# Scores of two heads in one step, with the low-part query products on the two row halves of the array

## The chip, the cores and the metric

The kernel runs on one core of a Trainium2 chip. The metric is device time in microseconds (us) from the start to the end of one execution. Where a trace is quoted, it comes from one profiled execution of the program.

## The reference

One layer of a hybrid encoder, for 1024 prompt frames and 64 frames that continue a stream with 512 cached frames. Every frame is normalised and projected to two attention branches and gates. Each branch has 8 heads of 64 channels. What the change touches are the scores, query times key over the 64 channels of a head, in both branches. Everything is float32.

```python
# stick-breaking branch ("sb")
z = jnp.einsum("bqhd,bkhd->bhqk", q, k).astype(jnp.float32) * ATTN_SCALE
causal = k_pos[None, :] < q_pos[:, None]
log_beta = jax.nn.log_sigmoid(z)
log_keep = jnp.where(causal, jax.nn.log_sigmoid(-z), 0.0)
suffix = lax.cumsum(log_keep, axis=3, reverse=True) - log_keep
w = jnp.where(causal, jnp.exp(log_beta + suffix), 0.0)
return jnp.einsum("bhqk,bkhd->bqhd", w.astype(v.dtype), v)
# band branch ("cb"): keys of the last 8 chunks of 64, softmax with a bias by distance
s = jnp.einsum("...qhd,...khd->...hqk", q, k).astype(jnp.float32) * ATTN_SCALE
```

Then both branch outputs are gated, projected, merged, projected again and added to the input.

## The kernel before, in words

**Split numbers.** A fast float32 product (the type `float32r`) keeps only part of the digits. So weights, activations, queries and keys are split into a high part and a low part, and a product is a sum of partial products. For the scores of one head the keys stand with the 64 rows of their high part and the 64 rows of their low part on the 128 rows of the array (tile `ks`, or `kss` for the 64 sample frames). The queries' high part stands twice, on both row halves, and so does their low part (tile `sq`, four planes: high and low of head 0, high and low of head 1). One matmul of 128 rows with the high part (line 725) gives high times high plus high times low; a second one with the low part (line 726) adds low times high plus low times low. Both go to the same PSUM tile `z` of one bank. `ks` and `sq` are filled by DMAs that `place_k` and `place_q` issue on SP's queue, `place_q` with four per tile.

**Phases.** Phase 1 (up to about 267 us of the trace) makes the normalised input and the natural-layout groups (line 357). Phases 2 and 3 (about 267 to 866 us) are one pipeline over all attention units, in which the matmuls of the remaining projections stand as fillers: `run_fill` and then `proj_units` give one filler matmul at a time (lines 563 and 661, up to 384 columns each). Phases 4 and 5 (to the end) are the rest of the projections and the output.

**Order of the attention pipeline.** The order on each engine is the order in which the program is written (`manual_schedule`). `seq` lists branch, pair of heads, query tile and head; query tile 8 is the 64 sample frames, tiles 0 to 7 have 128 prompt frames. A step is one query tile of one head. In step i, `qk(i)` computes the scores. Their width is 128 keys per query tile so far in the first branch (128 to 1024), 128 to 640 in the band branch, 576 for the sample frames. Widths over 512 are computed in two halves, in turn, with a `z` tile each; there are three `z` tiles. In the first branch ScalarE makes two sigmoids of each `z` (lines 728 and 729, tiles `kp` and `be`); in the band branch VectorE adds the bias and finds the extreme (line 731) and ScalarE takes the exponential (line 735). Then come half of the step's fillers, a pending `av` (values times weights, line 817, whose two heads stand on the two column halves of the array), `tr(i - 2)` (transposes of the weights, line 777, two PSUM tiles `pt`), `mid(i)` (first branch: the scan and a multiplication on VectorE, lines 745 and 746; band branch: the division, line 749), and the other half of the fillers. The number of fillers of a step follows the width of its scores.

**Buffers around it.** `be` has 3 buffers, `kp` 2, the band branch's small tile `sm` 4, `z` 3, `pt` 2. At the start of `qk` GpSimd writes one column of `kp` (line 716), which must wait until the buffer's former user is done. On GpSimd's queue the low parts of the filler weights (line 98) stand behind that.

Of the kernel before, what the change touches and what calls it, by code (L numbers as in the profile page):

```python
# [18 lines left out]
NP = 1024  # L19
# [11 lines left out]
def hybrid_step_kernel(ctx: ExitStack, tc: tile.TileContext, x_prompt, x_sample, c_sbk, c_sbv, c_cbk, c_cbv,  # L31
# [420 lines left out]
    def alloc_q(key, ci):  # L452
        if ci == 3:
            SQ[key, 3] = am.tile([128, 4, 64], F32R, name="sqs", bufs=1)
        else:
            n = min(CH[ci][1], NP) - CH[ci][0]
            SQ[key, ci] = am.tile([128, 4, n], F32R, name=f"sq{ci}", bufs=2 if ci == 2 else 1)
        return SQ[key, ci]
# [228 lines left out]
    def until(j):  # L687
        while prog[0] < j:
            next(gen)

# [1 line left out]
    seq = [(b, p, t, hd) for b in ("sb", "cb") for p in range(NPAIR) for t in [8] + list(range(8))  # L692
           for hd in range(2)]
# [9 lines left out]
    def qk(i):  # L703
        b, p, t, hd = seq[i]
# [4 lines left out]
        be = am.tile([128, NP], F32, name="be", bufs=3)  # L709
# [4 lines left out]
        if b == "sb":  # L714
            kp = ax.tile([128, NP + 2], F32, name="kp", bufs=2)
            G.memset(kp[:r, n:n + 1], 0.0)
        else:
            kp = am.tile([128, 4], F32, name="sm", bufs=4)
            bt = BI[2 * p + hd]
            off = 0 if t == 8 else 640 - n  # L720
        for j, (x, y) in enumerate(hs):
            z = psZ.tile([128, 512], F32, name="z")
            o = k0 * 128
            m = y - x
            TE.matmul(z[:r, :m], s[:, 2 * hd, q0:q0 + r], ks[:, hd, o + x:o + y], start=True, stop=False)  # L725
            TE.matmul(z[:r, :m], s[:, 2 * hd + 1, q0:q0 + r], ks[:, hd, o + x:o + y], start=False, stop=True)  # L726
            if b == "sb":
                A.activation(kp[:r, x:y], z[:r, :m], AF.Sigmoid, scale=-0.125)  # L728
                A.activation(be[:r, x:y], z[:r, :m], AF.Sigmoid, scale=0.125)
            else:  # L730
                V.tensor_tensor_reduce(be[:r, x:y], z[:r, :m], bt[:r, off + x:off + y], 1.0,  # L731
                                       BIG if j == 0 else kp[:r, j - 1:j], OP.add, OP.min, kp[:r, j:j + 1])
        if b == "cb":
            j = len(hs) - 1
            A.activation(be[:r, :n], be[:r, :n], AF.Exp, bias=kp[:r, j:j + 1], scale=-1.0, accum_out=kp[:r, 2:3])  # L735
        st[i] = (be, kp)

    def mid(i):
        b, p, t, hd = seq[i]
        r = rows(t)  # L740
        k0, n = band(b, t)
        be, kp = st[i]
        if b == "sb":
            im = imp[0:64, 960 - n:960] if t == 8 else imp[:, NP - n:NP]
            V.tensor_tensor_scan(kp[:r, n - 1::-1], kp[:r, n - 1::-1], im[:, ::-1], 0.0, op0=OP.mult, op1=OP.add)  # L745
            V.tensor_tensor(out=be[:r, :n], in0=be[:r, :n], in1=kp[:r, 1:n + 1], op=OP.mult)  # L746
# [9 lines left out]
    def tr(i):  # L756
        b, p, t, hd = seq[i]
        r = rows(t)
        k0, n = band(b, t)
        be, _ = st.pop(i)  # L760
# [64 lines left out]
    def prefetch(b, p, t):  # L825
        """Loads for the pair after (b, p), spread over its query tiles."""
# [38 lines left out]
    tot = {b: sum(wt[b](band(b, t)[1]) for bb, p, t, hd in seq if bb == b) for b in ("sb", "cb")}  # L865
    amount = {"sb": n_sb, "cb": n_cb}
    acc, emitted = 0.0, 0
    LAG = 2
    avq = []
    for i in range(len(seq) + LAG + 1):  # L870
        m = 0
        if i < len(seq):
            b, p, t, hd = seq[i]
            if b == "sb" and t == 8 and hd == 0:
                until(UK[p])
            if b == "cb" and p == 0 and t == 8 and hd == 0:
# [5 lines left out]
            qk(i)  # L882
            if hd == 0:
                prefetch(b, p, t)
            acc += amount[b] * wt[b](band(b, t)[1]) / tot[b]
            if (b, p, t) == ("cb", 0, 8):
                acc += 12
# [3 lines left out]
        fill(m // 2)  # L891
        while avq:
            av(*avq.pop(0))
        if 0 <= i - LAG < len(seq):
            tr(i - LAG)
            b, p, t, hd = seq[i - LAG]
            if hd == 1 and (t % 2 == 1 or t == 8):
# [129 lines left out]
```

## Time and profile before

| | |
|---|---|
| time, 3 runs | 1035.23, 1035.96 (median), 1036.86 us |
| span of the profiled execution | 1034.6 us |
| TensorE busy | 1014.8 us, 98% |
| weight loads busy (PEld) | 968.4 us, 94% |
| VectorE / ScalarE / GpSimd busy | 53% / 40% / 25% |
| granted TensorE clock | 0.999 |

The times lie some 1.4 us above the span, which runs from the first to the last instruction. Matmul durations in the profile are modelled from issue to the end of the drain, so consecutive ones overlap; how long a matmul holds the array is read from the distance between two starts. PE is TensorE's matmul, PEld its weight load, DVE is VectorE, ACT is ScalarE, POOL is GpSimd. Shapes such as `128*128 128x384` are weight rows times weight columns, and then the output.

### The profile page before, as it was taken

How to read it: one execution, taken by the hardware profiler on the slowest of the kernel's cores; microseconds unless marked ns; L12 is line 12 of the kernel's file. 1: busy time of each engine (PE TensorE's matmuls, PEld its weight loads, DVE VectorE, ACT ScalarE, POOL GpSimd, SP SyncE). 2: the span in 40 equal slices, each digit the busy share in tenths (PEclk: the TensorE clock that was granted, in tenths of full speed). 3: DMA queues.
4: the chain of work that ended last, by engine and by line, in shares of the span. 5: the costliest groups of instructions: out<-in, count | busy, mean ns of one | idle time of the engine just before them, and what ended most of it. 6: DMA issues, size and time to landing. Idle time of an engine off the chain costs nothing.

```text
span 1034.6 us, 19354 instructions
## 1 busy us (share of the span) xinstructions
PE 1014.8 (98%) x7412; PEld 968.4 (94%) x7412; DVE 543.9 (53%) x1069; ACT 418.7 (40%) x942; POOL 255.2 (25%) x277
## 2 busy tenths in 40 slices
PE   6999999999999999999999999999999999999998
PEld 5999999999999989999999999998988898999998
DVE  5416656402476556657655645565557685674111
ACT  5534443212454435444444454444445433552000
POOL 3227666202221111212121111101103211453110
PEclk9999999999999999999999999999999999999999
DMA  7654453745547323723384354665576834554322
GB/s 237 213 187 151 163 191 128 267 136 165 160 112 192 96 69 102 206 60 95 92 211 122 107 144 131 165 169 161 162 204 185 224 92 139 187 163 149 101 93 71
DMA packets 159660, 155.23 MB, mean 150 GB/s; under 512 B 23184, under 2 KB 144912, under 8 KB 159440
## 3 DMA queue, kind: packets, MB, share of 16 engines
q1 hardware_dynamic: 142800, 136.17, 44.2%
q10 hardware_dynamic: 16768, 17.83, 5.7%
q8 instruction: 58, 0.95, 0.4%
q14 instruction: 34, 0.28, 0.1%
HBM read 90.77 MB, written 49.81 MB: 136 GB/s over the span
## 4 chain that ended last, share of the span: by engine, by line
PE 91%; SPq 3%; DMA 2%; DVE 1%; ACT 1%; issue 1%; POOL 0%; ACTq 0%; DVEq 0%
PE acc L563 33%; PE acc L357 18%; PE acc L661 9%; PE o L817 7%; PE pt L777 6%; PE z L726 3%; PE z L725 3%; PE acc L992 3%; PE acc L991 3%; PE acc L990 3%; SPq L49 2%; DMA wrawx<-in_w_in_dram 1%; PE pk L301 1%; PE pt L229 1%; DMA d_ccbT<-hc 1%
## 5 line engine op out<-in xcount | busy, mean ns | idle before, releaser
L563 PE MATMUL acc<-xh,whi 128*128 128x384 f32 (+1 forms) x768 | 255.5, 333 | 0.1
L563 PE MATMUL acc<-xh,wlo 128*128 128x384 f32 (+1 forms) x768 | 255.3, 332 | 0.0
L563 PE MATMUL acc<-xl,whi 128*128 128x384 f32 (+1 forms) x768 | 254.8, 332 | 0.0
L98 POOL TENSOR_TENSOR wlo<-wraw,whi 128x1024 fp32r<-128x1024 f32 x51 | 127.6, 2501 | 440.2 <-ACT whi L91 386.1
L563 PEld LDWEIGHTS acc<-xh,wlo 128*128 128x128 f32 x768 | 144.8, 189 | 1.3
L563 PEld LDWEIGHTS acc<-xl,whi 128*128 128x128 f32 x768 | 144.5, 188 | 1.3
L563 PEld LDWEIGHTS acc<-xh,whi 128*128 128x128 f32 x768 | 144.5, 188 | 1.2 <-ACT sg L550 0.3
L745 DVE TENSOR_TENSOR_SCAN kp<-kp,imp 64x576 f32<-64x576 f32 (+8 forms) x72 | 110.6, 1536 | 5.1 <-ACT kp L728 5.1
L735 ACT ACTIVATE be<-be,sm 128x640 f32<-128x640 f32 (+5 forms) x72 | 50.8, 706 | 106.6 <-DVE sm L731 106.4
L728 ACT ACTIVATE kp<-z 128x384 f32<-128x384 f32 (+6 forms) x112 | 53.8, 480 | 97.3 <-PE z L726 87.6
L777 PE MATMUL pt<-ident,be 128*128 128x128 f32 (+2 forms) x608 | 88.8, 270 | 0.9 <-DVE wT L788 0.6
L786 ACT ACTIVATE wT<-pt 128x512 f32<-128x512 f32 (+3 forms) x104 | 52.9, 509 | 82.5 <-PE pt L777 81.6
L788 DVE COPY wT<-pt 128x256 f32<-128x256 f32 (+3 forms) x104 | 46.0, 442 | 70.3 <-PE pt L777 69.9
L777 PEld LDWEIGHTS pt<-ident,be 128*128 128x128 f32 (+2 forms) x608 | 68.7, 139 | 11.6 <-issue 7.1
L357 PE MATMUL acc<-whi,xh 128*128 128x256 f32 x256 | 75.2, 296 | 0.0
L357 PE MATMUL acc<-wlo,xh 128*128 128x256 f32 x256 | 71.7, 282 | 0.0
L357 PE MATMUL acc<-whi,xl 128*128 128x256 f32 x256 | 71.5, 281 | 0.0
L357 PE MATMUL acc<-whix,xh 128*128 128x256 f32 x256 | 70.9, 279 | 0.0
L357 PE MATMUL acc<-whix,xl 128*128 128x256 f32 x256 | 70.6, 278 | 0.0
L91 ACT ACTIVATE whi<-wraw 128x1024 fp32r<-128x1024 f32 x52 | 55.0, 1059 | 38.4 <-DVE y L996 35.8
L357 PE MATMUL acc<-wlox,xh 128*128 128x256 f32 x256 | 70.5, 277 | 0.0
L746 DVE TENSOR_TENSOR be<-be,kp 64x576 f32<-64x576 f32 (+8 forms) x72 | 62.3, 865 | 8.8
(157 smaller groups left out, 2168.7 us busy)
## 6 DMA issues: line engine op xcount, KB each, us to landing
wraw<-in_w_in_dram SPq DMA_DIRECT2D x40, 512.0 KB, 4.9
sq<-hl SPq DMA_DIRECT2D x32, 192.0 KB, 4.5
sq<-d_qT SPq DMA_DIRECT2D x32, 192.0 KB, 3.6
xt<-in_x_prompt_dram SPq DMA_DIRECT2D x8, 512.0 KB, 5.6
wrawx<-in_w_in_dram SPq DMA_DIRECT2D x8, 512.0 KB, 4.3
d_kT<-hl SPq DMA_DIRECT2D x8, 512.0 KB, 4.7
d_qT<-hl SPq DMA_DIRECT2D x8, 512.0 KB, 4.8
ks<-d_kT SPq DMA_DIRECT2D x16, 256.0 KB, 4.6
```

Source lines behind the costliest of these rows:

```text
L91: A.activation(h, raw, AF.Copy)
L98: (eng or G).tensor_tensor(out=l, in0=raw, in1=h[:].bitcast(F32), op=OP.subtract)
L357: TE.matmul(ps, x, w, start=m == 0, stop=m == len(steps) - 1)
L563: TE.matmul(ps[:, :b - a], w[:, k], xk(x, k)[:, a:b], start=k == 0 and n == 0, stop=k == KT - 1 and n == 2)
L661: TE.matmul(ps[:, :n], w[:, p, cw], g[:, a:e], start=p == 0 and m == 0, stop=p == NPAIR - 1 and m == 2)
L728: A.activation(kp[:r, x:y], z[:r, :m], AF.Sigmoid, scale=-0.125)
L735: A.activation(be[:r, :n], be[:r, :n], AF.Exp, bias=kp[:r, j:j + 1], scale=-1.0, accum_out=kp[:r, 2:3])
L745: V.tensor_tensor_scan(kp[:r, n - 1::-1], kp[:r, n - 1::-1], im[:, ::-1], 0.0, op0=OP.mult, op1=OP.add)
L746: V.tensor_tensor(out=be[:r, :n], in0=be[:r, :n], in1=kp[:r, 1:n + 1], op=OP.mult)
L777: TE.transpose(pt[:kr, x, :r], be[:r, kb * 128:kb * 128 + kr], ident[:r, :r])
L786: A.activation(w[:, sl:sl + m, q0:q0 + r], pt[:, :m, :r], AF.Copy)
L817: TE.matmul(o[hd * 64:hd * 64 + 64, c0:c1], vv[:kr, kb, hd * 64:hd * 64 + 64], wT[b, p, j, hd, s // 4][:kr, s % 4, c0:c1], start=si == 0, ...
```

## The change

A step now takes one query tile of both heads of a pair, so `seq` has 72 steps instead of 144. Of each part of the scores, first both heads' high-part products are issued, each on all 128 rows into a `z` tile of its own. Then come both low-part products, each on 64 rows only: low queries times the high part of the keys. Head 0 takes rows 0 to 63 of the array, head 1 rows 64 to 127. The product low times low is no longer computed. For this, `place_k` puts the high keys of head 1 on the lower row half, and `sq` has three planes, of which the third holds the low parts of both heads, one on each row half; `place_q` issues five DMAs instead of four, with three quarters of the bytes.

`qk` is a generator. Its first part runs at the start of a step, its second part (the second half of a wide tile, and the exponentials of the band branch) in the middle. A step's fillers stand in four groups, with `av`, the transposes of head 0 of the step before, the second part of the scores, the transposes of head 1, and `mid` for head 0 and head 1 between them. Transposes lag one step of both heads behind instead of two steps of one. `be` has 4 buffers, `sm` 6.

```diff
     def place_k(dst, h, o0, o1, a, b):
         rdma(dst[0:64, 0, a:b], h[0:64, 0, o0:o1])
         rdma(dst[64:128, 0, a:b], h[0:64, 1, o0:o1])
-        rdma(dst[0:64, 1, a:b], h[64:128, 0, o0:o1])
-        rdma(dst[64:128, 1, a:b], h[64:128, 1, o0:o1])
+        rdma(dst[0:64, 1, a:b], h[64:128, 1, o0:o1])
+        rdma(dst[64:128, 1, a:b], h[64:128, 0, o0:o1])
     def place_q(dst, h, o0, o1):
+        n = o1 - o0
         for hd in range(2):
             for dup in range(2):
-                rdma(dst[dup * 64:dup * 64 + 64, 2 * hd:2 * hd + 2, :o1 - o0], h[hd * 64:hd * 64 + 64, :, o0:o1])
+                rdma(dst[dup * 64:dup * 64 + 64, hd, :n], h[hd * 64:hd * 64 + 64, 0, o0:o1])
+        rdma(dst[:, 2, :n], h[:, 1, o0:o1])
...
         for j, (x, y) in enumerate(hs):
-            z = psZ.tile([128, 512], F32, name="z")
-            o = k0 * 128
             m = y - x
-            TE.matmul(z[:r, :m], s[:, 2 * hd, q0:q0 + r], ks[:, hd, o + x:o + y], start=True, stop=False)
-            TE.matmul(z[:r, :m], s[:, 2 * hd + 1, q0:q0 + r], ks[:, hd, o + x:o + y], start=False, stop=True)
...
+            zs = []
+            for hd in range(2):
+                z = psZ.tile([128, 512], F32, name="z")
+                TE.matmul(z[:r, :m], s[:, hd, q], ks[:, hd, o + x:o + y], start=True, stop=False)
+                zs.append(z)
+            for hd in range(2):
+                hp = slice(hd * 64, hd * 64 + 64)
+                TE.matmul(zs[hd][:r, :m], s[hp, 2, q], ks[hp, hd, o + x:o + y], start=False, stop=True)
...
         flush()
-        fill(m // 2)
+        fill(m // 4)
         while avq:
             av(*avq.pop(0))
-        if 0 <= i - LAG < len(seq):
-            tr(i - LAG)
...
+        if 0 <= i - 1 < len(seq):
+            tr(i - 1, 0)
+        fill(m // 4)
+        for _ in q:
+            pass
+        if 0 <= i - 1 < len(seq):
+            tr(i - 1, 1)
...
         if i < len(seq):
-            mid(i)
-        fill(m - m // 2)
+            mid(i, 0)
+        flush()
+        fill(m // 4)
+        if i < len(seq):
+            mid(i, 1)
+        fill(m - 3 * (m // 4))
```

TensorE's program of before, at the last prompt tile of the first pair of heads (scores 1024 wide, `z` the scores, `acc` a filler), has for one head:

```order
L563 MATMUL acc<-xl_134,whi 128x384
L725 MATMUL z<-ks,sq_3375 128x512
L726 MATMUL z<-ks,sq_3375 128x512
L725 MATMUL z<-ks,sq_3375 128x512
L726 MATMUL z<-ks,sq_3375 128x512
L563 MATMUL acc<-xh_132,wlo 128x384
```

All four are matmuls of 128 rows, and so are the fillers on both sides. The changed program has for the first half of both heads at that place (line 733 the high-part products, line 737 the two of 64 rows):

```order
L567 MATMUL acc<-xl_134,whi 128x384
L733 MATMUL z<-ks,sq_3377 128x512 x2
L737 MATMUL z<-ks,sq_3377 128x512 x2
L567 MATMUL acc<-xh_132,wlo 128x384
```

and for their second half, after two groups of fillers, ahead of the transposes of the step before (line 794):

```order
L567 MATMUL acc<-xh_131,whi 128x320
L733 MATMUL z<-ks,sq_3377 128x512 x2
L737 MATMUL z<-ks,sq_3377 128x512 x2
L794 MATMUL pt<-ident,be 128x128 x7
L567 MATMUL acc<-xh_131,wlo 128x320
```

Every pair of 64-row matmuls thus has matmuls of 128 rows on both sides. The program has 112 such pairs; 42 of them are followed by transposes, 70 by fillers.

On VectorE, the same query tile reads as follows before (lines 745 and 746 the scan and the multiplication of one head, 788 a copy of transposes):

```order
L788 COPY wT<-pt 128x3x128
L745 SCALAR_TENSOR_TENSOR kp<-kp,imp 128x1024
L746 TENSOR_TENSOR be<-be,kp 128x1024
L788 COPY wT<-pt 128x3x128
L745 SCALAR_TENSOR_TENSOR kp<-kp,imp 128x1024
L746 TENSOR_TENSOR be<-be,kp 128x1024
L544 TENSOR_TENSOR sg<-sg,acc 128x384
```

and now (762 and 763 are the scan and the multiplication, 805 the copy):

```order
L805 COPY wT<-pt 128x3x128 x2
L762 SCALAR_TENSOR_TENSOR kp<-kp,imp 128x1024
L763 TENSOR_TENSOR be<-be,kp 128x1024
L762 SCALAR_TENSOR_TENSOR kp<-kp,imp 128x1024
L763 TENSOR_TENSOR be<-be,kp 128x1024
L548 TENSOR_TENSOR sg<-sg,acc 128x384
```

The two copies of the step before now stand together ahead of both heads' scans, which follow each other directly.

More of the change, by code (lines that the diff above doesn't have):

```diff
@@ L453, in alloc_q @@
         if ci == 3:
-            SQ[key, 3] = am.tile([128, 4, 64], F32R, name="sqs", bufs=1)
+            SQ[key, 3] = am.tile([128, 3, 64], F32R, name="sqs", bufs=1)
         else:
             n = min(CH[ci][1], NP) - CH[ci][0]
-            SQ[key, ci] = am.tile([128, 4, n], F32R, name=f"sq{ci}", bufs=2 if ci == 2 else 1)
+            SQ[key, ci] = am.tile([128, 3, n], F32R, name=f"sq{ci}", bufs=2 if ci == 2 else 1)
         return SQ[key, ci]
@@ L689, in until @@
             next(gen)
-    seq = [(b, p, t, hd) for b in ("sb", "cb") for p in range(NPAIR) for t in [8] + list(range(8))
-           for hd in range(2)]
+    seq = [(b, p, t) for b in ("sb", "cb") for p in range(NPAIR) for t in [8] + list(range(8))]
     def band(b, t):
@@ L703, in qk @@
     def qk(i):
-        b, p, t, hd = seq[i]
+        b, p, t = seq[i]
         key = (b, p)
@@ L721, in qk @@
+        off = 0 if t == 8 else 640 - n
+        o = k0 * 128
         for j, (x, y) in enumerate(hs):
-            z = psZ.tile([128, 512], F32, name="z")
-            o = k0 * 128
             m = y - x
[L725 to L732, printed above, removed]
+            zs = []
[3 more added lines that the diff above has]
+                zs.append(z)
+            for hd in range(2):
+                hp = slice(hd * 64, hd * 64 + 64)
+                TE.matmul(zs[hd][:r, :m], s[hp, 2, q], ks[hp, hd, o + x:o + y], start=False, stop=True)
+            for hd in range(2):
+                z = zs[hd]
+                be, kp = st[i, hd]
+                if b == "sb":
+                    A.activation(kp[:r, x:y], z[:r, :m], AF.Sigmoid, scale=-0.125)
+                    A.activation(be[:r, x:y], z[:r, :m], AF.Sigmoid, scale=0.125)
+                else:
+                    V.tensor_tensor_reduce(be[:r, x:y], z[:r, :m], BI[2 * p + hd][:r, off + x:off + y], 1.0,
+                                           BIG if j == 0 else kp[:r, j - 1:j], OP.add, OP.min, kp[:r, j:j + 1])
+            yield
@@ L733, in qk, with mid @@
         if b == "cb":
             j = len(hs) - 1
[L735 to L739, printed above, removed]
+            for hd in range(2):
+                be, kp = st[i, hd]
+                A.activation(be[:r, :n], be[:r, :n], AF.Exp, bias=kp[:r, j:j + 1], scale=-1.0,
+                             accum_out=kp[:r, 2:3])
+    def mid(i, hd):
+        b, p, t = seq[i]
@@ L864, in hybrid_step_kernel @@
     wt = {"sb": lambda n: n, "cb": lambda n: n + 150}
-    tot = {b: sum(wt[b](band(b, t)[1]) for bb, p, t, hd in seq if bb == b) for b in ("sb", "cb")}
+    tot = {b: sum(wt[b](band(b, t)[1]) for bb, p, t in seq if bb == b) for b in ("sb", "cb")}
     amount = {"sb": n_sb, "cb": n_cb}
     acc, emitted = 0.0, 0
-    LAG = 2
     avq = []
-    for i in range(len(seq) + LAG + 1):
+    for i in range(len(seq) + 2):
         m = 0
+        q = iter(())
         if i < len(seq):
-            b, p, t, hd = seq[i]
-            if b == "sb" and t == 8 and hd == 0:
+            b, p, t = seq[i]
+            if b == "sb" and t == 8:
                 until(UK[p])
-            if b == "cb" and p == 0 and t == 8 and hd == 0:
+            if b == "cb" and p == 0 and t == 8:
                 sbx.close()
@@ L881, in hybrid_step_kernel @@
                 load_bias(1)
-            qk(i)
-            if hd == 0:
-                prefetch(b, p, t)
+            q = qk(i)
+            next(q)
+            prefetch(b, p, t)
             acc += amount[b] * wt[b](band(b, t)[1]) / tot[b]
             if (b, p, t) == ("cb", 0, 8):
-                acc += 12
+                acc += 24
             m = int(acc) - emitted
```

28 lines of the change are left out of this document (14 added, 14 removed).

## The prediction

> **What bounds the kernel now.** I read the page first, for the span and the chain that ended last, then busy time by stretches, then TensorE's timeline at the scores and wherever a matmul uses less than the whole array.
>
> ```profile
> span 1034.6 us, 19354 instructions
> PE acc L563 33%; PE acc L357 18%; PE acc L661 9%; PE o L817 7%; PE pt L777 6%; PE z L726 3%; PE z L725 3%; PE acc L992 3%; PE acc L991 3%; PE acc L990 3%; SPq L49 2%; DMA wrawx<-in_w_in_dram 1%; PE pk L301 1%; PE pt L229 1%; DMA d_ccbT<-hc 1%
> ```
>
> The chain runs through TensorE nearly all the time. The scores' two lines have 3% each. Next the stretches, two rows, with the stretch, its length, and busy time and count of PE, PEld, DVE, ACT and POOL, then clock, DMA share and GB/s:
>
> ```profile
> 267.00:636.00 369.00, 368.88 (x2482) 346.86 (x2483) 222.32 (x262) 169.34 (x382) 60.48 (x91) 1.00 0.43 120
> 636.00:866.00 230.00, 228.20 (x1650) 207.58 (x1648) 146.38 (x465) 105.48 (x252) 35.65 (x33) 1.00 0.62 174
> ```
>
> These are the attention in the first and in the band branch. TensorE idles 0.1 of 369 us and 1.8 of 230 us, the others have room. So the time of this stage is the sum of the distances between TensorE's starts, and what the change does to that sum it does to the kernel's time. Busy time itself doesn't show it: durations are modelled and overlap. Four starts of the scores show the distance (start, duration):
>
> ```profile
> 430.46 0.39 PE L725 MATMUL z<-ks,sq 128*128 128x512 f32 x1
> 430.69 0.40 PE L726 MATMUL z<-ks,sq 128*128 128x512 f32 x1
> 430.93 0.40 PE L725 MATMUL z<-ks,sq 128*128 128x512 f32 x1
> 431.16 0.40 PE L726 MATMUL z<-ks,sq 128*128 128x512 f32 x1
> ```
>
> Three distances make 0.70 us, 0.233 each, where the mean duration below is 0.395. The constant between them, 0.162 us, is the overlap: a matmul holds the array for its duration less 0.162.
>
> **What the change removes.** The groups of the low-part product, by shape (total busy us, mean ns):
>
> ```profile
> L726 PE MATMUL z<-ks,sq 128*128 128x320 f32 x80 | 24.0, 308 | 0.0
> L726 PE MATMUL z<-ks,sq 128*128 128x512 f32 x32 | 12.6, 395 | 0.0
> L726 PE MATMUL z<-ks,sq 128*128 128x384 f32 x32 | 10.8, 337 | 0.0
> L726 PE MATMUL z<-kss,sqs 128*64 128x288 f32 x32 | 8.9, 294 | 0.0
> L726 PE MATMUL z<-ks,sq 128*128 128x448 f32 x16 | 5.8, 366 | 0.0
> L726 PE MATMUL z<-ks,sq 128*128 128x256 f32 x16 | 4.5, 280 | 0.0
> L725 PE MATMUL z<-ks,sq 128*128 128x128 f32 x16 | 3.6, 222 | 0.0
> ```
>
> (The last row is the other line's, with the same number of matmuls, because a late weight load lengthens L726 there.) Less 0.162 each: 80 x 0.146 = 11.7, 32 x 0.233 = 7.5, 32 x 0.175 = 5.6, 32 x 0.132 = 4.2, 16 x 0.204 = 3.3, 16 x 0.118 = 1.9, 16 x 0.060 = 1.0: 35.2 us. If the two row halves run at once, a pair costs what one did: **-17.6 us**, or 0.157 for each of the 112 pairs.
>
> Do halves of the array run at once? The values' product uses the column halves, one head on each. Its rows, with six transposes on the whole array for the rate of plain float32:
>
> ```profile
> 365.67 0.31 PE L563 MATMUL acc<-xl,whi 128*128 128x320 f32 x1
> 365.91 3.46 PE L817 MATMUL o<-wT,vp 128*64 128x256 f32 x32
> 369.30 0.52 PE L777 MATMUL pt<-ident,be 64*128 64x64 f32 x5
> 426.86 0.82 PE L777 MATMUL pt<-ident,be 128*128 128x128 f32 x6
> ```
>
> The six take 0.82 with a last duration of 0.27, so 0.11 per 128 columns. The 32 products (28 of 256 columns, 4 of 128, by the program) would take 28 x 0.22 + 4 x 0.11 = 6.6 us in turn; from 365.91 to 369.30 they take 3.39. Column halves do run at once. That row halves do so too no run here shows; I take it by this row. The Trainium skill ("TensorEngine Tiling (Array Packing)", Key Properties) says that tiles load and multiply in parallel, row tiles included; by that the sum would be the same.
>
> **What it adds: 112 times from the whole array to row halves and back.** Before, scores and fillers all use 128 rows, and weights load behind the matmul in front. The one place with 64 rows in this stage are the transposes of the 64 sample frames. One such place, with scores of 128 keys ahead of it:
>
> ```profile
> 275.83 0.22 PE L725 MATMUL z<-ks,sq 128*128 128x128 f32 x1
> 275.89 0.28 PE L726 MATMUL z<-ks,sq 128*128 128x128 f32 x1
> 276.00 0.39 PE L563 MATMUL acc<-xh,whi 128*128 128x384 f32 x1
> 276.23 0.34 PE L563 MATMUL acc<-xl,whi 128*128 128x384 f32 x1
> 276.50 0.52 PE L777 MATMUL pt<-ident,be 64*128 64x64 f32 x5
> 276.94 0.44 PE L563 MATMUL acc<-xh,wlo 128*128 128x384 f32 x1
> 277.22 0.33 PE L563 MATMUL acc<-xh,whi 128*128 128x384 f32 x1
> 277.39 0.34 PE L563 MATMUL acc<-xl,whi 128*128 128x384 f32 x1
> ```
>
> and its weight loads:
>
> ```profile
> 276.49 0.36 PEld L777 LDWEIGHTS pt<-ident,be 64*128 64x128 f32 x5 [0.25 <-issue]
> 276.94 0.19 PEld L563 LDWEIGHTS acc<-xh,wlo 128*128 128x128 f32 x1
> 277.05 0.19 PEld L563 LDWEIGHTS acc<-xh,whi 128*128 128x128 f32 x1
> L777 PEld LDWEIGHTS pt<-ident,be 64*64 64x64 f32 x16 | 1.8, 110 | 0.0
> ```
>
> A filler of 384 columns holds the array 0.17 (277.22 to 277.39). The one ahead of the transposes holds it 0.27, and the weight load of the transposes starts only then, with them. The five loads are 0.36 long with a last one of 0.11, so 0.062 apart, and the transposes follow them. On the way back the filler's load again starts only with the filler (276.94), and that filler holds the array 0.28. From 276.23 to 277.22 it takes 0.99; without the two changes 0.17 + 5 x 0.062 + 0.17 = 0.65. The round trip costs 0.34. The same in phase 1, between matmuls of 256 columns, which hold 0.12:
>
> ```profile
> 82.28 0.28 PE L357 MATMUL acc<-wlox,xh 128*128 128x256 f32 x1
> 82.48 0.33 PE L301 MATMUL pk<-ident,qn 64*128 64x64 f32 x2
> 82.75 0.39 PE L357 MATMUL acc<-whi,xh 128*128 128x256 f32 x1
> 82.97 0.28 PE L357 MATMUL acc<-whi,xl 128*128 128x256 f32 x1
> ```
>
> 0.69 against 0.12 + 2 x 0.06 + 0.12 = 0.36: 0.33. I take 0.335. Every pair has 128-row work on both sides, so none shares a round trip: 112 x 0.335 = **+37.5 us**. The column halves show the way in as well: 0.24 from 365.67 to 365.91 for a filler that holds 0.147. The Trainium skill ("TensorEngine Tiling (Array Packing)", Key Properties) states that a change of tiling mode drains the engine, with no price; the trace agrees, and half of the 0.34 is a second thing, the load that can't go ahead.
>
> How long is the exposed load of a half? The trace's 64-row loads are 0.062 apart, whole ones 0.11 (276.94 to 277.05). If the second half's load waits for the first's, 0.062 more: 112 x 0.062 = 6.9 us; if both load at once, nothing. The column halves' pairs fit at once, I take nothing and keep 6.9 for the range. The Trainium skill ("TensorE: Matmul & The Clock Gate", LDWEIGHTS) holds that a load takes as long as its columns, whatever its rows. The trace differs, 0.062 for 64 rows against 0.11 for 128; by the page each way in would cost 0.05 more and the sum 5.6 us more.
>
> **Smaller terms.** With 128 keys, loads are late already: from 275.83 to 276.23 stand 0.06, 0.11 and 0.23 where 0.06, 0.06 and 0.17 would do. This 0.11 per head hides behind the change's own waiting: 16 x 0.11 = **-1.7 us**. 42 of the 112 pairs are followed by transposes, which themselves wait for loads; the exposed 0.11 on the way back may be covered there: 0 to -4.6, I take 0, since no row has this pair. One DMA more per query tile, 32 in all, goes to SP's queue ahead of the later key and value loads; TensorE's idle time of 0.1 + 1.8 us bounds what all DMAs cost the stage now, and a quarter more issues of one kind would add 0.5 at most. I take 0.
>
> **The other engines.** Per tile they do what they did. What is new is that both heads' scans stand behind each other, and that the second head's must end before the next tile's second `kp` is written and ScalarE can go on.
>
> ```profile
> L745 DVE TENSOR_TENSOR_SCAN kp<-kp,imp 128x1024 f32<-128x1024 f32 x8 | 19.9, 2489 | 0.0
> L746 DVE TENSOR_TENSOR be<-be,kp 128x1024 f32<-128x1024 f32 x8 | 9.8, 1226 | 0.9
> ```
>
> At the widest tile that is 2 x (2.49 + 1.23) = 7.4 us. Half a step lies between the second part of its scores and the next tile's first: by the step's share 38 fillers at 0.17, 6.5 us, and seven transposes, 0.8. Behind ScalarE's wait stand the evacuations of fillers, but a filler group of 24 lasts 4 us and has two buffers. I take 0.
>
> **Sum.** 1034.6 + 37.5 - 17.6 - 1.7 = 1052.8 for the span. The median run lies 1.4 above the span: **1054**.
>
> **Rivals.**
> 1. *The switch is free for float32r matmuls.* For: the score matmuls of the sample frames use 64 columns, and show no cost:
>
> ```profile
> 271.13 0.34 PE L563 MATMUL acc<-xh,wlo 128*128 128x384 f32 x1
> 271.30 0.29 PE L725 MATMUL z<-kss,sqs 128*64 128x288 f32 x1
> 271.43 0.29 PE L726 MATMUL z<-kss,sqs 128*64 128x288 f32 x1
> ```
>
> 0.17 and 0.13, as if nothing changed. The places that do pay are plain float32. Against: those columns start at 0 and have no neighbour on the other half, so the array need not be divided, while the change's second half starts at row 64; and 64 rows starting at 0 do pay. Then only the saving is left: 1034.6 - 17.6 - 1.7 + 1.4 = 1017. It decides from a round trip under 17.6 / 112 = 0.157 us; that is the drain of one way. Chance 0.07.
> 2. *The row halves do not run at once.* Their outputs leave through the same 128 columns, which the column halves' don't. Then the 17.6 doesn't come: 1054 + 17.6 = 1072. Chance 0.12.
> 3. *The scans are late.* If ScalarE stops long enough at the two widest tiles of each pair of heads, 8 places of 1 us (7.4 less 6.5): 1062. For it: GpSimd's and ScalarE's work of the next tile now waits for two scans in a row. Against: the two filler buffers, and that ScalarE and VectorE have room in both stretches. Chance 0.07.
>
> A change by which nothing happens (switching at just the price of the saving) has 0.02. The forecast keeps 0.72.
>
> **How the numbers follow.** Down from 1054: 4.6 for covered loads, 1.1 since 0.335 is read to 0.01, 0.7 for the runs' spread: 1047. Up: 6.9 for serial loads and 1.1: 1062, which holds rival 3 too. Since the ends are not sure, that is a little under 8 in 10, so I take in rival 2: 1047 to 1072. Faster by over 0.2% (about what a measurement of this kernel can tell from no change): 0.07; within: 0.02; slower: 0.72 + 0.12 + 0.07 = 0.91.
>
> **What would show it.** Line 737's two matmuls should start together or nearly so, with the weight loads of both starting with them and not behind line 733. The second high-part matmul should hold the array 0.09 longer than its columns, the first filler after a pair 0.11 longer. TensorE should still idle next to nothing between 267 and 880 us, and the added 18 us should lie in that stage alone. Wrong: loads of line 737 that go ahead during line 733 (rival 1); two starts of line 737 that stand 0.15 to 0.23 apart (rival 2); waits of TensorE for `be` or for ScalarE (rival 3).

## The result, and the profile after

| | before | changed |
|---|---|---|
| median of 4 runs | 1036.27 us (1035.23 to 1036.86) | 1067.04 us (1063.58 to 1068.5) |
| ratio, 95% interval | | 1.0287 (1.0264 to 1.031) |
| span of the profiled execution | 1034.6 us | 1066.7 us |
| granted TensorE clock there | 0.999 | 0.993 |

The kernel became 30.8 us slower. The forecast was 1054, 18 us slower, with a range to 1072: the direction and most of the mechanism held, and 13 us are missing from the sum. By its own terms the prediction's range ended at 1062; 1067 lies inside the stated range only because it was stretched to 1072 for rival 2, which the runs below rule out. That part of the hit is luck. The page of the changed kernel, the span and the chain that ended last:

```profile
span 1066.7 us, 19429 instructions
PE acc L567 32%; PE acc L357 17%; PE acc L665 7%; PE pt L794 7%; PE o L834 7%; PE z L737 4%; PE z L733 3%; PE acc L1017 3%; PE acc L1016 3%; PE acc L1018 3%; SPq L49 2%; DVE kp L762 1%; PE pk L301 1%; DMA wrawx<-in_w_in_dram 1%; PE pt L229 1%
```

TensorE still bounds it. The low-part line has 4% of a longer span instead of 3%, although two of its matmuls now share the time of one, and a VectorE scan (L762) stands in the chain with 1%, where before VectorE had no line. The place of the loss is the attention: the first matmul of phase 4 (L990, now L1016) starts at 959.57 instead of 928.9, so 30.7 of the 32.1 us of span are lost ahead of it, although the scores begin 1.1 earlier than they did.

The start of one 512-wide pair on TensorE, with a filler ahead and two behind (start, duration):

```profile
295.30 0.34 PE L567 MATMUL acc<-xh,wlo 128*128 128x384 f32 x1
295.48 0.63 PE L733 MATMUL z<-ks,sq 128*128 128x512 f32 x2
296.04 0.49 PE L737 MATMUL z<-ks,sq 64*128 64x512 f32 x2
296.46 0.45 PE L567 MATMUL acc<-xh,whi 128*128 128x384 f32 x1
296.74 0.34 PE L567 MATMUL acc<-xl,whi 128*128 128x384 f32 x1
```

and the weight loads of the same stretch:

```profile
295.30 0.36 PEld L733 LDWEIGHTS z<-ks,sq 128*128 128x128 f32 x2
296.03 0.19 PEld L737 LDWEIGHTS z<-ks,sq 64*128 64x128 f32 x2 [0.37 <-issue]
296.46 0.19 PEld L567 LDWEIGHTS acc<-xh,whi 128*128 128x128 f32 x1 [0.24 <-issue]
296.57 0.19 PEld L567 LDWEIGHTS acc<-xl,whi 128*128 128x128 f32 x1
```

The two matmuls of L737 are shown as one row of 0.49 us, about what one of them lasts (0.495 on average): they start 3 to 4 ns apart, so they do run at once. Their loads start with them, at 296.03, and the filler's load starts with the filler, at 296.46, while the next load (296.57) runs ahead again. That is the picture the prediction drew. The sizes are read from the starts. Undisturbed, two high-part matmuls hold 2 x 0.233 = 0.47, the pair 0.233, the filler 0.17. Here it is 0.56, 0.42 and 0.28. So the way in costs 0.09 behind the high parts, the pair 0.19 beyond its columns, and the first filler 0.11: **0.39 us** a round trip, where the prediction had 0.335.

Before transposes the same happens, cheaper at the end:

```profile
309.95 0.45 PE L733 MATMUL z<-ks,sq 128*128 128x320 f32 x2
310.33 0.41 PE L737 MATMUL z<-ks,sq 64*128 64x320 f32 x2
310.67 0.66 PE L794 MATMUL pt<-ident,be 128*128 128x128 f32 x4
311.09 0.42 PE L567 MATMUL acc<-xh,whi 128*128 128x384 f32 x1
```

The four transposes hold the array 0.42 (310.67 to 311.09). Four behind a filler hold it 0.36 (at 307.57 of this trace, with the next filler at 307.93), so the exposed load costs 0.06 there instead of 0.11.

The two stretches of the attention as in the prediction (stretch, its length, busy time and count of PE, PEld, DVE, ACT and POOL, clock, DMA share, GB/s), with ends moved to the longer run:

```profile
267.00:650.00 383.00, 380.00 (x2465) 336.30 (x2466) 215.66 (x261) 166.48 (x380) 60.32 (x91) 0.99 0.39 110
650.00:890.00 240.00, 237.39 (x1618) 199.29 (x1618) 140.27 (x453) 100.93 (x246) 36.15 (x33) 0.99 0.54 153
```

TensorE idles 3.0 and 2.6 us there, not next to nothing (0.1 and 1.8 before), and its clock, which was 1.00, is 0.99. Both are small; most of the idle time and all of the lower clock are new. The largest stall of the attention, on three engines around 280 us: first TensorE, then ScalarE, then VectorE.

```profile
280.13 0.51 PE L794 MATMUL pt<-ident,be 64*128 64x64 f32 x5 [1.44 <-ACT wT L803]
281.38 0.47 PE L567 MATMUL acc<-xh,whi 128*128 128x320 f32 x1
281.65 0.47 PE L567 MATMUL acc<-xl,whi 128*128 128x320 f32 x1
...
279.36 0.28 ACT L742 ACTIVATE kp<-z 128x128 f32<-128x128 f32 x1 [1.72 <-DVE be L763]
279.69 0.39 ACT L803 ACTIVATE wT<-pt 128x256 f32<-128x256 f32 x1
...
276.61 2.66 DVE L763 TENSOR_TENSOR be<-be,kp 64x576 f32<-64x576 f32 x1
```

The step is the narrow prompt tile behind the 64 sample frames. Read upwards: VectorE's multiplication for the sample frames' second head ends at 279.27. Until then ScalarE can't write the second head's `kp`, which has two buffers, and behind that sigmoid stands ScalarE's copy of finished transposes (L803). TensorE has both `pt` tiles full and waits 1.44 us for that copy. The two last TensorE rows show what follows: fillers of 320 columns 0.27 us apart, where they hold 0.146 at full rate. The windows at half rate in this trace, with the one ahead of the first:

```profile
274.00:280.60 6.60, 5.16 (x35) 4.27 (x33) 5.00 (x4) 2.77 (x9) 3.20 (x3) 1.00 0.52 142
280.60:287.40 6.80, 6.80 (x39) 5.79 (x39) 1.90 (x6) 2.20 (x7) 0.20 (x2) 0.50 0.08 29
659.40:662.80 3.40, 3.40 (x15) 3.40 (x14) 2.42 (x9) 2.48 (x6) 1.33 (x1) 0.50 0.95 267
963.20:966.60 3.40, 3.40 (x19) 3.40 (x18) 2.74 (x6) 1.82 (x4) 1.30 (x1) 0.50 0.92 307
```

For 6.8, 3.4 and 3.4 us the granted clock is 0.50. The third lies in phase 4, behind the attention. Before, no such window stands in the middle of the run.

### The profile page after: what moved, and what is told of

Same layout as the page of the kernel before. It is cut to its first block, busy times and chain, and to the rows that moved or that the text cites. A ratio compares the mean times of both kernels' runs of the same rounds, so it can differ in the third digit from the quotient of the medians.

```text
span 1066.7 us, 19429 instructions
## 1 busy us (share of the span) xinstructions
PE 1042.6 (98%) x7412; PEld 956.0 (90%) x7412; DVE 534.6 (50%) x1069; ACT 415.0 (39%) x942; POOL 255.3 (24%) x277
## 4 chain that ended last, share of the span: by engine, by line
PE 88%; DVE 3%; DMA 2%; SPq 2%; ACT 1%; issue 1%; POOL 1%; ACTq 0%; DVEq 0%; POOLq 0%
PE acc L567 32%; PE acc L357 17%; PE acc L665 7%; PE pt L794 7%; PE o L834 7%; PE z L737 4%; PE z L733 3%; PE acc L1017 3%; PE acc L1016 3%; PE acc L1018 3%; SPq L49 2%; DVE kp L762 1%; PE pk L301 1%; DMA wrawx<-in_w_in_dram 1%; PE pt L229 1%
## 5 line engine op out<-in xcount | busy, mean ns | idle before, releaser
L567 PE MATMUL acc<-xh,whi 128*128 128x384 f32 (+1 forms) x768 | 259.1, 337 | 0.0
L567 PE MATMUL acc<-xh,wlo 128*128 128x384 f32 (+1 forms) x768 | 258.0, 336 | 0.0
L567 PE MATMUL acc<-xl,whi 128*128 128x384 f32 (+1 forms) x768 | 257.5, 335 | 0.0
L762 DVE TENSOR_TENSOR_SCAN kp<-kp,imp 64x576 f32<-64x576 f32 (+8 forms) x72 | 109.4, 1520 | 5.9 <-ACT kp L742 5.9
L803 ACT ACTIVATE wT<-pt 128x512 f32<-128x512 f32 (+3 forms) x104 | 54.0, 519 | 129.6 <-PE pt L794 123.0
L794 PE MATMUL pt<-ident,be 128*128 128x128 f32 (+2 forms) x608 | 91.6, 275 | 4.3 <-DVE wT L805 1.7
L794 PEld LDWEIGHTS pt<-ident,be 128*128 128x128 f32 (+2 forms) x608 | 65.6, 139 | 21.5 <-issue 12.0
L834 PE MATMUL o<-wT,vp 128*64 128x256 f32 (+1 forms) x608 | 64.6, 356 | 0.0
```

Of the source, the lines that this page charges most:

```text
L567: TE.matmul(ps[:, :b - a], w[:, k], xk(x, k)[:, a:b], start=k == 0 and n == 0, stop=k == KT - 1 and n == 2)
L794: TE.transpose(pt[:kr, x, :r], be[:r, kb * 128:kb * 128 + kr], ident[:r, :r])
L803: A.activation(w[:, sl:sl + m, q0:q0 + r], pt[:, :m, :r], AF.Copy)
L834: TE.matmul(o[hd * 64:hd * 64 + 64, c0:c1], vv[:kr, kb, hd * 64:hd * 64 + 64], wT[b, p, j, hd, s // 4][:kr, s % 4, c0:c1], start=si == 0, ...
```

## The experiments

Two theories were to be told apart. The first: the round trip is dearer than forecast (0.38 instead of 0.335 us, for the reason that the exposed load is a full one), and the new order of the steps adds some 5 us of its own. The rival: the switch costs what was forecast, and the excess is stalls and a lower clock, brought by the order alone or by the row halves alone.

**The order without the row halves.** The changed kernel's order and buffers, with the low parts on 128 rows and the copies into `ks` and `sq` of before.

```diff
...
             for hd in range(2):
-                hp = slice(hd * 64, hd * 64 + 64)
-                TE.matmul(zs[hd][:r, :m], s[hp, 2, q], ks[hp, hd, o + x:o + y], start=False, stop=True)
+                TE.matmul(zs[hd][:r, :m], s[:, 2 * hd + 1, q], ks[:, hd, o + x:o + y], start=False, stop=True)
...
```

> The changed order (both heads in one step, fillers in four groups, five more buffers), but each low-part product on all 128 rows as before, so nothing is saved and the array never changes over for scores. Theory A (the array's change to row halves and back costs 0.34 to 0.40 us for each of 112 pairs, the new order next to nothing): 1036 to 1043 us, the clock at full rate throughout. Theory B (the new order costs the time: stalls of TensorE at the starts of the branches and half-rate stretches after them): 1055 us or more, with the same half-rate stretches as the changed kernel.

Measured: 1041.83 us (1038.41 to 1044.03, 9 runs) against 1036.74, ratio 1.0045 (1.003 to 1.0061). The order alone costs 5.1 us, a sixth of the loss. Its trace has one window at half rate, in phase 4 (937.1 to 940.5), and none in the attention. Its waits on TensorE sum to 21.2 us over the run, against 16.3 before and 20.5 in the changed kernel; the first rows of the attention in that view (waiting line, releaser, us in total, times, longest):

```profile
PE pt L789 <- DVE wT L800: 1.9, 2, 1.4
PE pt L789 <- ACT wT L798: 1.6, 1, 1.6
PE z L729 <- DVE sm L740: 1.3, 2, 0.9
```

and the start of the band branch, where the biases of both heads are needed in one step:

```profile
644.67 0.45 DVE L740 CUSTOM_DVE_ANT_0 be<-z,bias 64x288 f32<-64x288 f32 x1 [1.35 <-DMA bias<-d_rb]
645.05 0.68 DVE L800 COPY wT<-pt 128x512 f32<-128x512 f32 x1
645.78 0.66 PE L789 MATMUL pt<-ident,be 128*128 128x128 f32 x4 [1.36 <-DVE wT L800]
```

VectorE waits 1.35 us for a bias tile, the copy of transposes stands behind that wait, and TensorE waits 1.36 for the copy. So the stalls belong to the order of both heads in one step, not to the row halves.

**The switch without the saving.** Before's order, with one matmul of 64 rows and 64 keys ahead of each pair of high and low part of head 0, 112 in all. Its result is overwritten by the next matmul's `start`.

```diff
             m = y - x
+            if hd == 0:
+                TE.matmul(z[:r, :64], s[0:64, 1, q0:q0 + r], ks[0:64, 0, o + x:o + x + 64], start=True, stop=True)
             TE.matmul(z[:r, :m], s[:, 2 * hd, q0:q0 + r], ks[:, hd, o + x:o + y], start=True, stop=False)
```

> The kernel before, with one extra matmul of 64 rows and 64 columns ahead of the scores of head 0 of each part (112 in all); the scores overwrite its result. Theory A: each costs 0.09 to drain, 0.05 to 0.10 for its exposed load, 0.03 to 0.06 itself, 0.09 to drain again and 0.11 for the exposed load behind it: 0.37 to 0.45 us, 1078 to 1087 us in all. Theory B: an extra matmul costs its columns, 0.06 us, 1043 us in all.

Measured: 1079.18 us (1078.4 to 1080.68), ratio 1.0408 (1.0393 to 1.0424), which is 42.4 us or 0.379 us for each.

```profile
290.95 0.34 PE L563 MATMUL acc<-xh,wlo 128*128 128x384 f32 x1
291.22 0.29 PE L726 MATMUL z<-ks,sq 64*128 64x64 f32 x1
291.44 0.50 PE L727 MATMUL z<-ks,sq 128*128 128x512 f32 x1
291.78 0.39 PE L728 MATMUL z<-ks,sq 128*128 128x512 f32 x1
292.01 0.34 PE L563 MATMUL acc<-xh,whi 128*128 128x384 f32 x1
```

0.27 for a filler that holds 0.17, 0.22 for the little matmul, 0.34 for a matmul of 512 columns that holds 0.233. The granted clock was 1.0. So switching alone lowers no clock, and it costs this much in an order that is otherwise before's.

**The same matmul on 128 rows.**

```diff
-                TE.matmul(z[:r, :64], s[0:64, 1, q0:q0 + r], ks[0:64, 0, o + x:o + x + 64], start=True, stop=True)
+                TE.matmul(z[:r, :64], s[:, 1, q0:q0 + r], ks[:, 0, o + x:o + x + 64], start=True, stop=True)
```

> As e2_before_plus_112_half_matmuls, but the 112 extra matmuls of 64 columns use all 128 rows: no switch. If the switch is the price, each costs only the 0.05 to 0.11 that its load takes: 1042 to 1050 us. If any extra short matmul costs 0.38, 1079 us.

Measured: 1046.87 us (2 runs), ratio 1.0098 (1.0063 to 1.0134), 10.5 us or 0.09 each. An extra matmul of 64 keys costs 0.09; with 64 rows instead of 128 it costs 0.29 more. Most of the price is that of the row half, not of an extra instruction. The 0.29 is less than the 0.39 above, because so short a matmul doesn't cover the next load with 128 rows either: the 512-wide matmul behind it holds the array 0.31 there (289.29 to 289.60) instead of 0.233.

**One half alone.** The changed kernel without head 1's low-part product, which is left out of its scores.

```diff
-                TE.matmul(z[:r, :m], s[:, hd, q], ks[:, hd, o + x:o + y], start=True, stop=False)
+                TE.matmul(z[:r, :m], s[:, hd, q], ks[:, hd, o + x:o + y], start=True, stop=hd == 1)
                 zs.append(z)
-            for hd in range(2):
+            for hd in range(1):
```

> The changed kernel without head 1's low-part product; head 0's stands alone on rows 0 to 63. If the two halves run at once, this saves nothing that lasts: within 5 us of the changed kernel's 1067, the distance from the half's start to the next matmul as before. The load exposed ahead of it tells two cases apart: 0.10 us again if a load takes as long as its 128 columns, 0.05 us if the two halves' loads stood one behind the other (then 112 x 0.05 = 6 us faster).

Measured: 1068.1 us (2 runs), ratio 1.03 (1.0279 to 1.0321), the changed kernel's time.

```profile
296.00 0.63 PE L733 MATMUL z<-ks,sq 128*128 128x512 f32 x2
296.56 0.49 PE L737 MATMUL z<-ks,sq 64*128 64x512 f32 x1
296.98 0.44 PE L567 MATMUL acc<-xh,whi 128*128 128x384 f32 x1
```

One matmul holds the array 0.42, as two on both halves do. The second half is free, its matmul and its load. So the 0.19 beyond the columns isn't two loads in turn: it is one load of 0.11 (the distance between loads at 296.46 and 296.57 above) and 0.08 to 0.09 of a wait like the 0.09 on the way in. The prediction reads these waits as the array's drain; the trace shows their time, not what happens in it.

**Both on the same half.** Head 1's low part takes rows 0 to 63 too, with head 0's low queries and the low-half keys of its own plane, so its low part is another product than the reference's.

```diff
-                hp = slice(hd * 64, hd * 64 + 64)
+                hp = slice(0, 64)
```

> The changed kernel with both low-part products on rows 0 to 63 (head 1 with head 0's low queries and keys). If it is the two halves that let them run at once, here they stand one behind the other: the second starts 0.06 to 0.23 us after the first by its columns, 17.6 us more in all, about 1084 us. If the pair overlaps for another reason (an array that takes two short products anyway), 1067 us.

Measured: 1080.76 us (2 runs, 1077.4 and 1084.11), ratio 1.0422 (1.038 to 1.0464), 13.7 us over the changed kernel. The distances around the scores sum to 16.3 us more. The traces of the two kernels differ in the clock, 0.999 here and 0.993 there, so the distances tell more than the times.

```profile
292.33 0.63 PE L733 MATMUL z<-ks,sq 128*128 128x512 f32 x2
292.89 0.73 PE L737 MATMUL z<-ks,sq 64*128 64x512 f32 x2
293.55 0.45 PE L567 MATMUL acc<-xh,whi 128*128 128x384 f32 x1
```

0.66 from 292.89 to 293.55 instead of 0.42: one 512-column matmul more, 0.233. Over all scores the parallel halves thus bring 16.3 of the 17.6 us that the prediction took by columns.

**The saving alone.** The order on 128 rows, without head 1's low-part product, which is left out of its scores: a pair costs one low-part matmul and no switch.

```diff
-                TE.matmul(z[:r, :m], s[:, 2 * hd, q], ks[:, hd, o + x:o + y], start=True, stop=False)
+                TE.matmul(z[:r, :m], s[:, 2 * hd, q], ks[:, hd, o + x:o + y], start=True, stop=hd == 1)
                 zs.append(z)
-            for hd in range(2):
+            for hd in range(1):
                 TE.matmul(zs[hd][:r, :m], s[:, 2 * hd + 1, q], ks[:, hd, o + x:o + y], start=False, stop=True)
```

> The changed order on the whole array (as in e1_pair_steps_whole_rows, 1041.8 us), without head 1's low-part product. This takes away what the change saves, with no switch paid for it: 35.2 / 2 = 17.6 us less by the sum of the prediction, 1024 us. If less than 12 us go, the saving term was too large and the switch is cheaper than its 0.38 us; if TensorE were not the bound, nothing would go.

Measured: 1027.35 us (1026.38 to 1030.35), ratio 0.9915 (0.9888 to 0.9941), 14.5 us under the order alone. The distances around the scores fell by 17.4 us, as expected. 3 us came back elsewhere: TensorE's waits rose from 21.2 to 23.2, and a window at half rate appeared behind the stall near 279 us, without a row half in its scores (the sample frames' transposes have 64 rows in every one of these kernels):

```profile
279.00:285.80 6.80, 6.61 (x41) 5.88 (x42) 1.90 (x6) 2.29 (x9) 0.20 (x2) 0.50 0.09 31
```

**One more `kp` buffer.** The changed kernel, so that ScalarE's sigmoid of the second head need not wait for the step before.

```diff
-                kp = ax.tile([128, NP + 2], F32, name="kp", bufs=2)
+                kp = ax.tile([128, NP + 2], F32, name="kp", bufs=3)
```

> The changed kernel with three kp buffers instead of two, so that the first sigmoid of a tile's second head waits for the first head's multiplication of the tile before, not for the second head's. If the stall of 1.6 us on the narrow tile behind the first sample tile, and with it the 6.8 us at half rate right behind, come from that wait: the stall falls below 1 us, the half-rate stretch at 281 us goes, 3 to 6 us in all, 1061 to 1064 us. If the half rate comes from the row halves themselves: 1066 to 1068 us, the stretch stays.

Measured: 1064.69 us (1061.42 to 1065.5), ratio 1.0264 (1.0236 to 1.0292). That is 2.4 us less in the median, a little short of the 3 to 6 expected, and the two intervals overlap. The trace is plainer than the time:

```profile
279.13 0.49 PE L794 MATMUL pt<-ident,be 64*128 64x64 f32 x5 [0.72 <-DVE be L763]
...
280.60:287.40 6.80, 6.80 (x58) 5.79 (x57) 3.37 (x9) 2.71 (x9) 0.30 (x3) 1.00 0.17 53
654.90:658.30 3.40, 3.40 (x15) 3.40 (x14) 2.33 (x9) 2.48 (x6) 1.24 (x1) 0.51 0.95 270
```

The stall is 0.72 instead of 1.44, and the same 6.8 us that ran at 0.50 run at 1.00, with 58 matmuls in place of 39. The window at the start of the band branch, whose stall has another cause, is still there, as is the one in phase 4.

**Is a load short because of 64 rows, or because of the type?** The prediction had read the load of a half, 0.062, from plain float32 transposes. Here the 112 extra matmuls are plain float32.

```diff
-                TE.matmul(z[:r, :64], s[0:64, 1, q0:q0 + r], ks[0:64, 0, o + x:o + x + 64], start=True, stop=True)
+                TE.matmul(z[:r, :64], s[0:64, 1, q0:q0 + r].bitcast(F32), ks[0:64, 0, o + x:o + x + 64].bitcast(F32),
+                          start=True, stop=True)
```

> As e2_before_plus_112_half_matmuls (1079.2 us), but the 112 extra matmuls read the same data as plain float32 instead of float32r. If the exposed load of a half depends on the type (0.05 for plain float32, 0.10 for float32r, whatever the rows): 112 x 0.05 less, 1073 to 1074 us, with weight loads of 0.14 instead of 0.18 in the trace. If it depends on the rows, the load is the same: 1079 us or a little more.

Measured: 1093.05 us (1092.59 to 1094.44), ratio 1.0548 (1.0519 to 1.0577), 13.9 us over the float32r version, which neither side expected. The groups of matmuls and of their loads (total us, mean ns):

```profile
L726 PE MATMUL z<-ks,sq 64*128 64x64 f32 x192 | 41.5, 296 | 0.0
L726 PEld LDWEIGHTS z<-ks,sq 64*128 64x128 f32 x192 | 28.3, 184 | 22.1 <-issue 20.0 <-DVE sm L751 0.7 <-DVE be L752 0.4
```

The program has 96 such products on prompt frames, and the trace 192 matmuls with 192 loads: a plain float32 product is issued as two. Each load lasts 184 ns, as the float32r ones of 64 rows do in the changed kernel, against 138 to 189 in these rows of its groups:

```profile
L794 PEld LDWEIGHTS pt<-ident,be 128*128 128x128 f32 x528 | 59.9, 141 | 16.6 <-issue 10.6 <-DVE wT L805 2.2 <-ACT ko L531 0.7
L794 PEld LDWEIGHTS pt<-ident,be 64*128 64x128 f32 x64 | 5.1, 138 | 4.9 <-ACT wT L803 3.0 <-issue 1.4 <-ACT wT L799 0.5
L733 PEld LDWEIGHTS z<-ks,sq 128*128 128x128 f32 x192 | 34.2, 189 | 0.9 <-DVE sm L745 0.9
L737 PEld LDWEIGHTS z<-ks,sq 64*128 64x128 f32 x192 | 18.0, 184 | 21.7 <-issue 19.5 <-DMA gt<-d_gsb 0.4 <-DMA kss<-d_csbT 0.3
```

Transposes load in 141 and 138 ns, with 128 rows and with 64; matmuls in 189 and 184, with 128 rows and with 64. At 128 columns, what sets the short load is the transpose, neither the rows nor the type.

**All pairs ahead of transposes.** Since the exit into transposes is cheaper, the first part of the scores is moved behind `av`, so that 110 of the 112 pairs end there; once with the row halves and once with 128 rows in the same order.

```diff
             q = qk(i)
-            next(q)
-            prefetch(b, p, t)
...
             av(*avq.pop(0))
+        if i < len(seq):
+            next(q)
+            prefetch(b, p, t)
         if 0 <= i - 1 < len(seq):
```

> The changed kernel, but the first part of a step's scores comes behind its first group of fillers and the pending values' product, right ahead of the transposes of head 0: 110 of 112 pairs of halves are then followed by transposes instead of 42. The way back to a transpose exposes 0.056 us of load, to a filler 0.109: 68 x 0.053 = 3.6 us less. The sample tile's scores also start a quarter step later, so that the query and bias DMAs have more time, and stalls at the starts of the branches, with the half-rate stretches behind them, may go too: 1058 to 1064 us against 1067. If the exposed load is the same whatever follows: 1065 us or more.

> The same move of the first part of the scores in the order on the whole array (e1_pair_steps_whole_rows, 1041.8 us). No switch is paid, so only stalls can change: if the 5 us of the new order lie in DMAs and biases that come late for two heads at once at the starts of the branches, 1037 to 1040 us; if in the doubled steps of VectorE and ScalarE, 1041 to 1045 us.

Measured: 1060.2 us (1058.52 to 1062.04) with the halves, ratio 1.0225 (1.0203 to 1.0248), and 1043.07 (1041.96 to 1044.14) with whole rows, ratio 1.0059 (1.0045 to 1.0072). The stretches with the halves:

```profile
267.00:650.00 383.00, 379.60 (x2492) 336.60 (x2491) 216.22 (x261) 166.84 (x384) 59.55 (x91) 1.00 0.39 111
650.00:890.00 240.00, 236.80 (x1642) 198.73 (x1641) 141.40 (x466) 103.16 (x252) 37.16 (x34) 1.00 0.54 157
```

The clock is 1.00 in both, with all 112 switches in the program, and the kernel is 6.8 us faster than the changed one. The exits were to bring 3.6 of them; the median run's clock, 0.999 against 0.9955, is worth about 3.7. The move didn't take the order's own stalls away: with whole rows it has 1043.07 us against 1041.83 without the move. The two runs differ by the row halves alone (with the DMAs that fill their tiles), by 17.1 us. From 110 round trips of 0.343, two of 0.396, and the savings of 17.6 and 1.7 come 38.5 - 19.3 = 19.2; where the 2.1 us between the two go isn't shown.

## Why the prediction was right, and where its sum was short

The pieces of the 30.8 us: the order, 5.1 (measured alone). The row halves: all distances around the scores, with the excess of the first instructions behind them, sum to 74.0 us in the order alone and to 97.8 in the changed kernel, 23.8 more. Together 28.9; the 1.9 left are put down to the half-rate windows by their size alone, since 0.0025 of granted clock (0.9955 against 0.998 in the middle run) is 2.7 us of 1067. Against the sum of the prediction, the 13 us that are missing are thus 5.1 for the order, 4.6 for dearer round trips, some 2 for the clock and 1 that no term explains.

**The term that was mis-sized: "How long is the exposed load of a half?"** The prediction took 0.062 us for 64 rows and counted the round trip at 0.335, both from plain float32 transposes of 64 rows, in the attention and in phase 1. It named the cause, a load that can't go ahead, rightly, and its size from the wrong instruction. The load of a matmul with 128 columns takes 0.105 to 0.11 whatever its rows. Measured at 128 columns, a round trip is 0.09 (drain in) + 0.105 (load) + 0.088 (drain out) + 0.11 (load behind), where the 0.19 that the pair takes beyond its columns is split by taking the load as 0.105. Over all widths it is about 0.396 for the 70 pairs that fillers follow and 0.343 for the 42 that transposes follow: 42.1 us instead of 37.5. The sample frames' pairs load 64 columns instead of 128; their loads last 129 ns, and such a pair takes only 0.14 beyond its columns (at 657.08, with the next start at 657.35 and 0.131 for 288 columns). The rows to see the size were in before's trace, among its groups of weight loads:

```profile
L563 PEld LDWEIGHTS acc<-xh,whi 128*128 128x128 f32 x768 | 144.5, 188 | 1.2 <-ACT sg L550 0.3
L777 PEld LDWEIGHTS pt<-ident,be 128*128 128x128 f32 x528 | 63.0, 140 | 8.4 <-issue 4.1 <-DVE wT L788 0.8 <-ACT wT L786 0.5
L777 PEld LDWEIGHTS pt<-ident,be 64*128 64x128 f32 x64 | 5.2, 138 | 3.3 <-issue 3.0 <-ACT kp L728 0.2
```

The transposes' loads last 140 ns with 128 rows and 138 with 64, a filler's 188: these rows spoke against a load that is short because it has half the rows. The Trainium skill ("TensorE: Matmul & The Clock Gate", LDWEIGHTS) holds that a load's time goes by its columns and not by its rows. The prediction set this aside for the trace, and gave 5.6 us as what the sum would be short by it. The measurement agrees with the page here: 184 ns with 64 rows, 189 with 128; the loads of transposes, shorter at the same columns, it doesn't explain.

**Exits into transposes**, taken at 0 with a bound of -4.6: -2.2 (42 x 0.053), which the 42.1 holds already. A half-covered load, inside the bound.

**The saving of 17.6 and 1.7: right, within about a us.** Both halves start together, the second is free (one half alone: no change), on one half they cost 16.3 more, and the whole-array order without the second product had 17.4 less. The 1.7 was not measured by itself. The price sum by its own steps is 37.5 + 4.6 - 19.3 = 22.8, against 23.8 measured. The evidence that the prediction gave was weaker than it read. It counted 32 products on the column halves by the program; the program has 16 there, each issued as two matmuls, and the rate in turn came from transposes, which are issued once. The starts in that trace do show column halves at once: they stand 7 ns apart in pairs, with about 0.216 us from one pair of 256 columns to the next. That row halves run at once is shown by the runs with one half and with both on the same one. Rival 2 (in turn, 1072) is dead, though the time came within 5 us of it: without the traces, the total would have spoken for the wrong cause.

**"The other engines ... I take 0": wrong by 5.1 us.** The prediction looked for rival 3 at the widest tiles, where 7.4 us of scans stand against 7.3 of TensorE's work. There TensorE doesn't wait. The stalls come at the narrowest step, behind the sample frames, where few fillers stand between and VectorE still works on the wider step before, and at the start of the band branch, where both heads' biases are needed at once. Rival 3's mechanism (ScalarE held by `kp`, TensorE by ScalarE's copies) is the right one for the first, at another place and about a fifth of its price.

**The clock: not foreseen.** The half-rate windows cost 2 to 3 us more than in the order alone, an estimate from the clocks of the median runs above.

**The signs named in advance.** L737's matmuls start together: yes. Their loads start with them: yes. The second high part holds 0.09 longer: 0.094. The first filler 0.11 longer: 0.109. TensorE idles next to nothing: no, 5.6 us. The loss lies in the attention alone: nearly, 30.7 of 32.1 us stand ahead of phase 4, and a half-rate window stands behind its start.

What stays open. What exactly brings the clock to a half: the windows of the changed kernel follow stalls of 1.44, 1.15 and 2.2 us, one went when its stall was halved, and switching alone brought none. But the same lengths stand elsewhere without a window behind them: 1.8 us in before's trace (ahead of L991), 1.7 and 2.2 in the run with all pairs ahead of transposes. And whether the halves pay when several pairs share a switch: at 0.157 us saved per pair on average it takes 0.376 / 0.157 = 2.4 pairs a switch to break even, 0.376 / 0.233 = 1.6 at 512 keys, both estimates. That needs more than the three `z` tiles, and wasn't tried.

## What to carry to other kernels

A change from the whole array to row halves and back costs about 0.4 us here with float32r matmuls of 128 weight columns: two waits of 0.09, which the prediction calls drains, and two weight loads of 0.11 that don't run ahead, so it pays only where a stay on the halves saves more than that: here a stay saved 0.16. Take the price of an operation from rows of the same kind of instruction: a transpose's load isn't a matmul's. And when a step is made twice as large, look for late engines at the narrowest step behind a wide one, not at the widest, where fillers cover most.

## What the runs showed that I had not expected

- Weight loads of 128 columns last 138 to 141 ns for transposes and 184 to 190 ns for matmuls, float32r and plain float32 alike, with 64 rows or 128.
- A plain float32 product is issued as two matmuls with a load each: 192 rows for 96 products, and 0.12 us more per product (13.9 us over 112) for 64 keys.
- TensorE's granted clock can fall to 0.50 for 3.4 or 6.8 us in a kernel that is 98% busy, behind stalls of 1.15 to 2.2 us, though not behind each of that length.
- Two matmuls on the two row halves start 3 to 4 ns apart and cost what one does.
